# A transformer and state-space layer: its feed-forward network by seven products of quarter blocks, with normed input and stored activations

## The chip, the core and the metric

The kernel runs on one core of a Trainium2 chip. The metric is the device time of one execution in microseconds; lower is better.

## The reference

One layer on 1024 tokens with 1024 channels, all in fp32. Attention heads and a state-space (SSD) mixer run side by side, and their outputs are projected back and added to x. Then comes the feed-forward part, which is what the change touches:

```
x = x + jnp.concatenate([y_ssd, y_att], axis=-1) @ w_out[l]
h = rms_norm(x, norm2_w[l])
x = x + (jax.nn.silu(h @ w_gate[l]) * (h @ w_up[l])) @ w_down[l]
```

`w_gate` and `w_up` are 1024 x 2816, `w_down` is 2816 x 1024; 2816 is 22 tiles of 128.

## The kernel before

Channels lie on the 128 partitions, tokens along the free dimension. A matrix operand in fp32 is taken as a sum of two fp32r numbers: a high part, which ScalarE copies (line 136 for weights), and a low part, the difference of the two, by VectorE or GpSimd (line 137). A product is then three matmuls: high by high, high by low, low by high. `mm3` (lines 142 to 147) does that for both halves of 512 tokens at once, in six matmuls of 128x512 into two PSUM banks.

Attention runs to about 545 us, the SSD mixer to about 860, and the output projection to about 1004. Its eight tiles of 128 channels are added by `add_out` and `add_last`, and its operands are split by `split_y` (lines 887 and 888). `out_post` adds the two banks to x in `x2[d]` (lines 996 and 997), and ScalarE and GpSimd sum the squares (line 1005). As each `x2[d]` is done, it is multiplied by the norm's weight and split into `xh` and `xl` (lines 1015 and 1016), not yet by the norm's factor, which hangs on all channels.

In the feed-forward part `gate_up(f)` makes one tile of 128 of the 2816 channels: 8 tiles of x, gate and up, so 16 `mm3` and 96 matmuls. The factor of the norm (`norm2`, made while the first tile runs) goes on the products when they leave PSUM (lines 1050 and 1052). VectorE and ScalarE then form silu(gate) times up, and split it in turn (lines 1054 and 1055). `down(f0, n, ...)` multiplies four such tiles (two in the last part) with `w_down` and adds to `x2`: 8 output tiles of 6n matmuls. Parts are interleaved so that a `down` has the next `gate_up` ahead of it. The last output tile goes in columns of 512, 256 and 256 (`tail`, line 1059). GpSimd does nothing here after the norm's power (line 100).

A scheduler of the compiler sets the order of instructions on each engine from the program's order and from when its model takes operands to be ready; pools with a given number of buffers (`bufs`) make a writer wait for the readers of an older tile. Loads of weights are issued by SyncE (SP); loads of x by GpSimd (line 989).

Of the kernel before, what the change touches and what calls it, by code (L numbers as in the profile page):

```python
# [24 lines left out]
FF_PARTS = [(0, 4), (4, 4), (8, 4), (12, 4), (16, 4), (20, 2)]  # L25
# [40 lines left out]
def layer(ctx, tc, xT, wq0, wqkv, wxz, wout, wgu, wdn, pk, pb, cst, rot, sel, out):  # L66
# [44 lines left out]
    def row_a(spread):  # L111
        for i in range(2):
# [9 lines left out]
    def row_b(bank, spread, dst):  # L122
        for i in range(2):
# [760 lines left out]
    def split_y(src, pl_, tag, eng):  # L884
        yh = pl_.tile([P, S], F32R, tag=tag, name="yh", bufs=16)
        yl = pl_.tile([P, S], F32R, tag=tag, name="yl", bufs=16)
        A.copy(out=yh, in_=src)
# [299 lines left out]
```

## Time and profile before

| | |
|---|---|
| median of 3 runs | 1730.51 us (1730.05 to 1730.52) |
| the profiled execution | 1730.91 us, of which the span is 1729.1 |
| TensorE matmul (PE) | 1692.8 us busy (98%), 8614 matmuls |
| VectorE (DVE) | 956.2 us (55%) |
| ScalarE (ACT) | 679.2 us (39%) |
| GpSimd (POOL) | 443.7 us (26%) |
| moved by DMA | 93.5 MB, mean 54 GB/s |

The span is the profiled part of one execution; 1.8 us lie around it. Busy shares are means over the whole span; what a change does is read from the stretches that it touches. The mean duration of a matmul in the groups, some 393 ns, is the time from its start to its end, and matmuls overlap in the engine: the pace is read from how many go by in a stretch.

### The profile page before, as it was taken

Reading aid. Unit: us, or ns where it says so; the run is one execution under the profiler, and the core shown is the slowest. Engines: PE = TensorE matmul, PEld = TensorE weight load, DVE = VectorE, ACT = ScalarE, POOL = GpSimd, SP = SyncE. Lnnn points to the kernel's source line nnn. Section 1 sums busy time; section 2 is a strip of 40 time slices with the busy share of each in tenths; the row PEclk is TensorE's granted clock in tenths of the full one; section 3 lists DMA queues with packets and bytes.
Section 4 is the critical chain, followed back from the end, with each engine's and each line's share of the span. In section 5 each row is a group of like instructions: output and inputs, shape, how many; then the busy total and the mean of one; then the engine's idle time right before and its main releaser. Section 6 shows DMA issues by size and latency. Waiting matters only on the chain.

```text
span 1729.1 us, 23256 instructions
## 1 busy us (share of the span) xinstructions
PE 1692.8 (98%) x8614; PEld 1445.6 (84%) x8614; DVE 956.2 (55%) x1969; ACT 679.2 (39%) x1517; POOL 443.7 (26%) x678
## 2 busy tenths in 40 slices
PE   7899999999999999999999999999999999999999
PEld 7799999999988787887778788888888888888887
DVE  7788888878886577877531333333333333333334
ACT  5576666666664445447221322112112112212211
POOL 5755665566511334334242100000000000000000
PEclk8899999999999999999999999999999999999999
DMA  5100110111011111132141111111111111111112
GB/s 183 38 25 26 49 44 22 35 49 32 13 42 35 47 37 37 52 132 98 50 146 46 46 49 44 36 61 49 37 56 49 43 56 49 43 50 49 49 48 112
DMA packets 50033, 93.50 MB, mean 54 GB/s; under 512 B 5738, under 2 KB 14442, under 8 KB 49920
## 3 DMA queue, kind: packets, MB, share of 16 engines
q1 hardware_dynamic: 39024, 82.44, 14.5%
q10 hardware_dynamic: 9504, 4.72, 1.0%
q0 software_dynamic: 1392, 4.85, 0.8%
q8 instruction: 68, 1.11, 0.3%
q14 instruction: 45, 0.37, 0.1%
HBM read 81.51 MB, written 10.49 MB: 53 GB/s over the span
## 4 chain that ended last, share of the span: by engine, by line
PE 67%; DVE 1%; POOL 0%; issue 0%; ACT 0%; DVEq 0%; POOLq 0%
PE p L142 9%; PE p L143 9%; PE p L147 9%; PE p L145 9%; PE p L144 8%; PE p L146 8%; PE ps_x L461 4%; PE ps_x L462 4%; PE ps_x L463 4%; PE ps_y L797 1%; PE ps_n L775 1%; PE ps_o L813 1%; PE ps_d L752 1%; PE ps_xt L741 0%; DVE yl L888 0%
## 5 line engine op out<-in xcount | busy, mean ns | idle before, releaser
L136 ACT CAST wh<-wr 128x512 fp32r<-128x512 f32 (+3 forms) x237 | 153.1, 647 | 708.6 <-PE p L145 604.1
L137 DVE TENSOR_TENSOR wl<-wr,wh 128x512 fp32r<-128x512 f32 (+1 forms) x175 | 130.1, 743 | 274.7 <-ACT wh L136 274.7
L184 PE MATMUL ps_pj<-wh,xwh 128*128 128x384 f32 (+1 forms) x512 | 176.1, 347 | 6.9 <-ACT wh L136 6.1
L186 PE MATMUL ps_pj<-wh,xwl 128*128 128x384 f32 (+1 forms) x512 | 174.2, 342 | 3.9 <-DVE xwl L251 3.9
L185 PE MATMUL ps_pj<-wl,xwh 128*128 128x384 f32 (+1 forms) x512 | 174.4, 341 | 0.0
L137 POOL TENSOR_TENSOR wl<-wr,wh 128x512 fp32r<-128x512 f32 (+3 forms) x62 | 101.8, 1642 | 236.0 <-ACT wh L136 229.0
L142 PE MATMUL p<-xh,wh 128*128 128x512 f32 x352 | 138.6, 394 | 0.7 <-DVE x L996 0.7
L143 PE MATMUL p<-xl,wh 128*128 128x512 f32 x352 | 138.8, 394 | 0.0
L144 PE MATMUL p<-xh,wh 128*128 128x512 f32 x352 | 138.6, 394 | 0.0
L145 PE MATMUL p<-xl,wh 128*128 128x512 f32 x352 | 138.3, 393 | 0.0
L147 PE MATMUL p<-xh,wl 128*128 128x512 f32 x352 | 138.3, 393 | 0.0
L146 PE MATMUL p<-xh,wl 128*128 128x512 f32 x352 | 137.7, 391 | 0.0
L461 PE MATMUL ps_x<-xwh,wh 128*128 128x512 f32 x320 | 129.2, 404 | 0.8 <-ACT ya L405 0.8
L462 PE MATMUL ps_x<-xwl,wh 128*128 128x512 f32 x320 | 126.2, 394 | 0.0
L463 PE MATMUL ps_x<-xwh,wl 128*128 128x512 f32 x320 | 125.7, 393 | 0.0
L359 ACT ACTIVATE pt<-ps_s,nm 128x640 f32<-128x640 f32 (+7 forms) x128 | 94.3, 740 | 45.1 <-DVE nm L354 26.3
L184 PEld LDWEIGHTS ps_pj<-wh,xwh 128*128 128x128 f32 x512 | 97.8, 191 | 7.7 <-ACT wh L136 7.2
L186 PEld LDWEIGHTS ps_pj<-wh,xwl 128*128 128x128 f32 x512 | 97.5, 191 | 5.0 <-DVE xwl L251 4.9
L185 PEld LDWEIGHTS ps_pj<-wl,xwh 128*128 128x128 f32 x512 | 97.6, 191 | 0.8 <-POOL wl L137 0.4
L354 DVE TENSOR_REDUCE nm<-ps_s 128x1 f32<-128x640 f32 (+7 forms) x128 | 93.4, 744 | 1.2
L1082 DVE TENSOR_TENSOR x<-p,x 128x512 f32<-128x512 f32 x47 | 32.1, 689 | 110.3 <-PE p L146 110.3
L142 PEld LDWEIGHTS p<-xh,wh 128*128 128x128 f32 x352 | 66.1, 188 | 15.6 <-ACT wh L136 1.4
(238 smaller groups left out, 3850.0 us busy)
## 6 DMA issues: line engine op xcount, KB each, us to landing
wr<-in_wgu_dram SPq DMA_DIRECT2D x88, 256.0 KB, 2.7
wr<-in_wdn_dram SPq DMA_DIRECT2D x44, 256.0 KB, 2.7
wr<-in_wqkv_dram SPq DMA_DIRECT2D x28, 384.0 KB, 3.1
wr<-in_wxz_dram SPq DMA_DIRECT2D x40, 256.0 KB, 2.7
wr<-in_wout_dram SPq DMA_DIRECT2D x32, 256.0 KB, 2.8
big<-yd SPq DMA_DIRECT2D x10, 512.0 KB, 3.8
yd<-ya ACTq DMA_DIRECT2D x64, 64.0 KB, 1.7
x<-in_xT_dram POOLq DMA_DIRECT2D x8, 512.0 KB, 6.3
```

Source lines behind the costliest of these rows:

```text
L137: lo_eng.tensor_tensor(out=wl[:, cs], in0=wr[:, cs], in1=wh[:, cs], op=ALU.subtract)
L142: T.matmul(out=ps0, lhsT=wh, rhs=ah[:, 0:512], start=first, stop=False)
L143: T.matmul(out=ps0, lhsT=wh, rhs=al[:, 0:512], start=False, stop=False)
L144: T.matmul(out=ps1, lhsT=wh, rhs=ah[:, 512:1024], start=first, stop=False)
L145: T.matmul(out=ps1, lhsT=wh, rhs=al[:, 512:1024], start=False, stop=False)
L146: T.matmul(out=ps0, lhsT=wl, rhs=ah[:, 0:512], start=False, stop=last)
L147: T.matmul(out=ps1, lhsT=wl, rhs=ah[:, 512:1024], start=False, stop=last)
L184: T.matmul(out=ps[:, :n], lhsT=xwh[k][:, ts], rhs=wh[:, k % 2, :], start=k == first, stop=False)
L185: T.matmul(out=ps[:, :n], lhsT=xwh[k][:, ts], rhs=wl[:, k % 2, :], start=False, stop=False)
L186: T.matmul(out=ps[:, :n], lhsT=xwl[k][:, ts], rhs=wh[:, k % 2, :], start=False, stop=k == last)
L461: T.matmul(out=ps, lhsT=wh[:, ks], rhs=xwh[k][:, fs], start=k == 0, stop=False)
L462: T.matmul(out=ps, lhsT=wh[:, ks], rhs=xwl[k][:, fs], start=False, stop=False)
```

## The change

A product of two 2x2 block matrices takes eight products of blocks. The change does it in seven (`PRODUCTS`), with four sums of weight blocks and four of data blocks formed beforehand, and the seven results added up into the four blocks of the output. For gate and up the blocks are: data, the halves of the tokens by the halves of the channels (a11, a12, a21, a22); weights, gate and up by the halves of the channels. For the down product: halves of the tokens by the two tiles of a pair, and two output tiles.

- **x normed first.** Only normed x can be summed. The output projection's last two tiles are done for the first half of the tokens, then for the second, with their weights loaded twice; after each half `norm2(hf)` makes the factor, multiplies eight tiles of x by it (line 1059) and splits them (`split`, lines 152 and 153). x before the norm is stored to DRAM (`x2d`).
- **Two tiles plainly, twenty by seven products.** Tiles 0 and 1 go as before, one half after the other, while GpSimd forms the sums of x (lines 1077 to 1083). `GateUp` does a tile in seven products of 12 matmuls. GpSimd forms the four sums of weights (line 1151); VectorE forms the low halves and, with ScalarE, adds up the results.
- **Activations through DRAM.** `store_pair` writes three quarters of each pair of activation tiles and four sums of them (GpSimd, lines 1096 to 1102) to `md`, 77 blocks of 256 KB.
- **The down product last, in four chunks** of 3, 3, 3 and 2 pairs. A chunk has four steps, one for each pair of output tiles, of 7 products with 3n matmuls each. `fetch_m` loads the blocks of a chunk (line 1264) into four buffers `mr` and splits them; `Ahead` does it for the next chunk between the products of the last step. The sums start from x, loaded from `x2d` (line 1325).

```diff
-FF_PARTS = [(0, 4), (4, 4), (8, 4), (12, 4), (16, 4), (20, 2)]
+NPLAIN = 2
+CHUNKS = [(0, 3), (3, 3), (6, 3), (9, 2)]
+PRODUCTS = ["a11", "s2", "s1", "s3", "a12", "s4", "a22"]
+BANKS = "abcdacd"
...
+    def split(op, src, eng, n=512):
+        A.copy(out=op[:, 0:n], in_=src)
+        eng.tensor_tensor(out=op[:, n : 2 * n], in0=src, in1=op[:, 0:n], op=ALU.subtract)
+        return op
...
-    def mm3(ps0, ps1, wh, wl, ah, al, first, last):
+    def mm3(ps, wh, wl, a, first, last, more=False):
+        T.matmul(out=ps, lhsT=wh, rhs=a[:, 0:512], start=first, stop=False, skip_group_check=more)
+        T.matmul(out=ps, lhsT=wh, rhs=a[:, 512:1024], start=False, stop=False, skip_group_check=more)
+        T.matmul(out=ps, lhsT=wl, rhs=a[:, 0:512], start=False, stop=last, skip_group_check=more)
...
+            for hf in range(2):
+                for d in range(DK - 2, DK):
+                    for hq in range(4):
+                        add_out(d, hq // 2, hq % 2, (hf,))
+                jobs.append((lambda ws, hf=hf: norm2(hf), []))
...
+    def out_post(d, hf):
+        fs = halves[hf]
+        V.tensor_tensor(out=x2[d][:, fs], in0=pd.pop((d, hf)), in1=x2[d][:, fs], op=ALU.add)
+        nc.sync.dma_start(out=x2d[d, :, fs], in_=x2[d][:, fs])
...
+    def norm2(hf):
...
+        row_b(bank, [sx], accm[:, fs])
+        for d in range(DK):
...
+            V.scalar_tensor_tensor(out=x2[d][:, fs], in0=x2[d][:, fs], scalar=nw, in1=accm[:, fs], op0=ALU.mult, op1=ALU.mult)
+            name = f"a{1 + hf}{1 + d // 4}"
+            op = (rb if name in ("a11", "a22") else ra).tile([P, S], F32R, tag=name, name=name, bufs=4)
+            ops[(name, d % 4)] = split(op, x2[d][:, fs], V)
...
+    def store_pair(i):
...
+        G.tensor_tensor(out=s3, in0=m0[:, 0:512], in1=m0[:, 512:1024], op=ALU.subtract)
+        put("s3", s3)
...
     while jobs:
         half()
+    for f, u, hf, last in ((0, 0, 0, 0), (0, 1, 0, 0), (1, 0, 0, 0), (0, 0, 1, 1), (0, 1, 1, 1), (1, 0, 1, 1), (1, 1, 0, 0), (1, 1, 1, 1)):
+        if (f, u, hf) == (0, 1, 1):
...
+                    ops[(name, k)] = split(op, src, V)
+        plain(f, u, hf, last)
...
+    class Weights:
...
+                G.tensor_tensor(out=self.t[name], in0=x, in1=y, op=ALU.subtract)
...
+    class GateUp:
...
+        def product(self, j):
...
+            ps, w = self.ps[BANKS[j]], self.parts[j]
+            for k in range(4):
+                mm3(ps, w[:, k * P : (k + 1) * P], w[:, 512 + k * P : 512 + (k + 1) * P], ops[(PRODUCTS[j], k)], k == 0 and j < 4, k == 3, j > 3)
...
+            elif j == 5:
+                m = m_tile(self.f)[:, halves[0]]
+                add(m, self.u)
+                V.tensor_tensor(out=m, in0=m, in1=self.g0, op=ALU.mult)
+            else:
+                g1 = mq.tile([P, 512], F32, tag="gt", name="gt", bufs=2)
+                add(g1, self.u)
+                A.activation(g1, g1, AF.Silu)
+                V.tensor_tensor(out=m_tile(self.f)[:, halves[1]], in0=self.up1, in1=g1, op=ALU.mult)
...
+    def run(steps):
...
+        for n, st in enumerate(steps):
+            for j in range(7):
+                st.product(j)
+                if n + 1 < len(steps):
+                    steps[n + 1].prepare(j)
+                if n + 2 < len(steps) and j in (3, 6):
+                    steps[n + 2].load((0, 1) if j == 3 else (2, 3))
+            st.end()
...
+    def fetch_m(c, j):
+        p0, n = CHUNKS[c]
+        for i in range(n):
+            mr = wd.tile([P, 512], F32, tag="mr", name="mr", bufs=4)
+            nc.gpsimd.dma_start(out=mr, in_=md[p0 + i, j])
+            mo[(c, j, i)] = split(rd.tile([P, S], F32R, tag="op", name="mo", bufs=24), mr, V)
...
+    class Down:
...
+            wr = wd.tile([P, 3, 4, P], F32, tag="wr", name="wr", bufs=2)[:, : self.n]
+            nc.sync.dma_start(out=wr, in_=wdn[self.p0 : self.p0 + self.n, self.d].rearrange("i p (q n) -> p i q n", n=P))
...
+            A.copy(out=op[:, 0], in_=src)
+            V.tensor_tensor(out=op[:, 1], in0=src, in1=op[:, 0], op=ALU.subtract)
...
+            for i in range(self.n):
+                mm3(ps, w[:, 0, i], w[:, 1, i], mo[(self.c, j, i)], i == 0 and j < 4, i == self.n - 1, j > 3)
...
+    for j in range(7):
+        fetch_m(0, j)
     for d in range(DK):
...
+        nc.gpsimd.dma_start(out=acc[d], in_=x2d[d])
+
+    class Ahead(Down):
+
+        def product(self, j):
+            super().product(j)
+            if not self.last:
+                fetch_m(self.c + 1, j)
+
+    run([(Ahead if d == DK // 2 - 1 else Down)(c, d) for c in range(len(CHUNKS)) for d in range(DK // 2)])
```

**TensorE where the feed-forward begins.** Before (`xh`, `xl`: split x; `wh`, `wl`: split weights; `yh`: the projection's operand; `p`: a PSUM bank):

```order
L147 MATMUL p_10364<-yh,wl 128x512
L142 MATMUL p_10523<-xh,wh 128x512
L143 MATMUL p_10523<-xl,wh 128x512
L144 MATMUL p_10524<-xh,wh 128x512
L145 MATMUL p_10524<-xl,wh 128x512
L146 MATMUL p_10523<-xh,wl 128x512
L147 MATMUL p_10524<-xh,wl 128x512
L142 MATMUL p_10523<-xh,wh 128x512
```

After, at the second half (`op`: split weights; `a`: split x, high and low in one tile):

```order
L166 MATMUL p_10683<-a_10409,op 128x512
L117 MATMUL ps_tr<-cst_sb,wide 40x128
L135 MATMUL ps_bc<-sx,ones_r 128x512
L164 MATMUL p_10710<-a_10568,op 128x512
L164 MATMUL p_10805<-a_10568,op 128x512
L164 MATMUL p_10831<-a_10568,op 128x512
L165 MATMUL p_10710<-a_10568,op 128x512
L166 MATMUL p_10710<-a_10568,op 128x512
```

Before, the first matmul on x follows the last of the projection. Now a transpose and a broadcast of the norm's factor stand between them, and three tiles take turns with the second half of x as its tiles come.

**VectorE at the same place.** Before:

```order
L996 TENSOR_TENSOR x_7_9725<-p_10363,x_7_9725 128x512
L997 TENSOR_TENSOR x_7_9725<-p_10364,x_7_9725 128x512
L137 TENSOR_TENSOR wl<-wr,wh 128x512
L1016 SCALAR_TENSOR_TENSOR xl<-x_7_9725,pk_sb,xh 128x1024
L137 TENSOR_TENSOR wl<-wr,wh 128x512 x2
L99 TENSOR_SCALAR rtok<-ps_r_10573 128x8
L105 COPY wide<-rtok 128x2x8
```

After (`sx`: the factor's spread rows; `m`: an activation tile; `accm`: the factor on all partitions):

```order
L123 TENSOR_TENSOR sx<-wrow,cst_sb 40x512
L1122 TENSOR_TENSOR m<-p_10646,gt 128x512
L1059 SCALAR_TENSOR_TENSOR x_0_9701<-x_0_9701,pk_sb,accm 128x512
L1059 SCALAR_TENSOR_TENSOR x_1_9703<-x_1_9703,pk_sb,accm 128x512
L1059 SCALAR_TENSOR_TENSOR x_2_9705<-x_2_9705,pk_sb,accm 128x512
L1059 SCALAR_TENSOR_TENSOR x_3_9707<-x_3_9707,pk_sb,accm 128x512
L1059 SCALAR_TENSOR_TENSOR x_4_9709<-x_4_9709,pk_sb,accm 128x512
L1059 SCALAR_TENSOR_TENSOR x_5_9711<-x_5_9711,pk_sb,accm 128x512
L1059 SCALAR_TENSOR_TENSOR x_6_9713<-x_6_9713,pk_sb,accm 128x512
L1059 SCALAR_TENSOR_TENSOR x_7_9715<-x_7_9715,pk_sb,accm 128x512
L153 TENSOR_TENSOR a_10568<-x_0_9701,a_10568 128x512
```

Before, only the last tile's addition and its low half stand ahead of that first matmul, and the norm comes behind. Now all eight tiles are normed first, and the first low half (line 153) comes behind the eighth.

**GpSimd from the output projection to the end, and from gate-up to down.** Before, its last rows:

```order
L1005 TENSOR_TENSOR accm<-accm,sq_10351 128x512
L1005 TENSOR_TENSOR accm<-accm,sq_10354 128x512
L1005 TENSOR_TENSOR accm<-accm,sq_10469 128x512
L1005 TENSOR_TENSOR accm<-accm,sq_10472 128x512
L100 TENSOR_TENSOR rtok<-rtok,mhalf 128x8
L1183 UNCONDITIONAL_BRANCH
L1183 ISA
```

After, where gate-up passes to down (`sd`: the last activation sum; `mr`: an activation block; `acc`: x to add to; `t`: a weight sum):

```order
L1102 TENSOR_TENSOR sd<-m,sd 128x512
L1264 DMA mr<-md 128x512 x4
L1325 DMA acc_13880<-x2d 128x1024
L1325 DMA acc_13881<-x2d 128x1024
L1325 DMA acc_13882<-x2d 128x1024
L1325 DMA acc_13883<-x2d 128x1024
L1325 DMA acc_13884<-x2d 128x1024
L1325 DMA acc_13885<-x2d 128x1024
L1325 DMA acc_13886<-x2d 128x1024
L1325 DMA acc_13887<-x2d 128x1024
L1151 TENSOR_TENSOR t<-wr 128x384
L1264 DMA mr<-md 128x512 x4
```

Before, there is nothing for it in the feed-forward part. Now the issue of the first block loads stands behind the last sum, four can go, eight loads of x come next, and the other blocks stand behind these.

## Rows read from the trace of the kernel before

Groups of lines give engine, operation, out<-in, form and count, then busy us, mean ns of one, and idle us just before with what ended most of it. Chains and timelines give start us, us, and what.

**Rows 1.** Windows: output projection, a feed-forward stretch, the end.

```profile
core 0: us, PE busy (x) PEld busy (x) DVE busy (x) ACT busy (x) POOL busy (x), PEclk, DMA share, GB/s
870.00:980.00 110.00, 110.00 (x480) 89.99 (x479) 24.27 (x30) 27.82 (x40) 31.07 (x26) 1.00 0.24 81
1112.47:1245.15 132.68, 132.68 (x577) 108.50 (x577) 46.22 (x72) 24.71 (x40) 0.00 (x0) 1.00 0.15 48
1643.66:1729.10 85.44, 81.66 (x360) 66.75 (x359) 32.98 (x53) 9.90 (x16) 0.00 (x0) 1.00 0.22 80
```

**Rows 2.** Waits of PE after 780 us: us, times, longest us.

```profile
PE p L143 <- POOL yl L888: 1.3, 1, 1.3
PE p L142 <- DVE x L996: 0.7, 1, 0.7
```

**Rows 3.** Chain that ended last, around 862 us (start us, us, what).

```profile
861.27 1.06 ACT yh L887
862.40 3.47 POOL yl L888
```

**Rows 4.** Groups by line and form: busy us, mean ns | idle before.

```profile
L463 PE MATMUL ps_x<-xwh,wl 128*128 128x512 f32 x320 | 125.7, 393 | 0.0
L1055 DVE TENSOR_TENSOR ml<-ut,mh 128x512 fp32r<-128x512 f32 x44 | 28.5, 689 | 1.9
L845 DVE SCALAR_TENSOR_TENSOR big<-big,pk_sb,accg 128x1024 f32<-128x1024 f32 x8 | 11.9, 1542 | 6.2 <-ACT accg L126 6.2
L136 ACT CAST wh<-wr 128x512 fp32r<-128x512 f32 x204 | 126.2, 620 | 705.4 <-PE p L145 604.1 <-PE ps_x L462 49.1 <-issue 13.7
L989 POOL DMA_DIRECT2D x<-in_xT_dram x8 | 4.4, 554 | 2.6 <-DVE yl L888 2.6
L299 POOL TENSOR_TENSOR raw<-raw,w_qk 128x192 f32<-128x192 f32 x56 | 41.1, 734 | 76.5 <-ACT raw L298 45.8 <-issue 29.7 <-POOL klo L336 0.9
```

**Rows 5.** Timeline and groups, 600 to 800 us: DVE beside POOL.

```profile
649.18 2.54 POOL L757 TENSOR_TENSOR mt<-mt,cbt 128x512 f32<-128x512 f32 x2 [0.45 <-ACT mt L756]
650.82 1.45 DVE L137 TENSOR_TENSOR wl<-wr,wh 128x512 fp32r<-128x512 f32 x1 [2.43 <-ACT wh L136]
...
L822 DVE TENSOR_TENSOR big<-big,eac 128x384 f32<-128x384 f32 x7 | 6.2, 884 | 0.2
L821 DVE TENSOR_TENSOR eac<-ps_o,eac 128x384 f32<-128x384 f32 x7 | 3.9, 555 | 0.0
```

**Rows 6.** Line 137 from 1112 to 1643 us: duration ns min/median/max.

```profile
L137 DVE TENSOR_TENSOR wl<-wr,wh x96: 680/691/696, 1124.3 to 1637.7; 128x512 fp32r<-128x512 f32 x96
```

**Rows 7.** Windows around a wait near 32 us, columns as rows 1.

```profile
30.00:32.00 2.00, 0.81 (x3) 0.48 (x3) 2.00 (x1) 0.83 (x1) 1.63 (x1) 1.00 0.09 37
32.00:34.00 2.00, 0.04 (x1) 0.04 (x1) 2.00 (x3) 0.00 (x0) 0.00 (x0) 0.88 0.60 190
34.00:36.00 2.00, 2.00 (x6) 1.99 (x7) 1.92 (x2) 0.00 (x0) 0.00 (x0) 0.50 0.03 10
40.00:45.00 5.00, 5.00 (x20) 4.96 (x19) 4.15 (x17) 1.76 (x5) 4.89 (x12) 0.62 0.00 0
```

**Rows 8.** Chain around the start of the feed-forward.

```profile
1003.83 1.68 PE ps_r L98 x16
1016.78 0.66 PE ps_bc L125 x2
```

**Rows 9.** DMA issues (KB each, median us to landing), and a window.

```profile
wr<-in_wgu_dram SPq DMA_DIRECT2D x88, 256.0 KB, 2.7
x<-in_xT_dram POOLq DMA_DIRECT2D x8, 512.0 KB, 6.3
out_dram<-x SPq DMA_DIRECT2D x2, 128.0 KB, 2.1
sel_f<-in_sel_dram POOLq DMA_DIRECT2D x2, 120.0 KB, 2.8
...
10.00:15.00 5.00, 5.00 (x28) 4.77 (x27) 4.26 (x9) 4.62 (x6) 4.89 (x9) 1.00 1.04 408
```

More of the change, by code (lines that the diff above doesn't have):

```diff
@@ L111, in row_a @@
     def row_a(spread):
-        for i in range(2):
+        for i in range(len(spread)):
             V.tensor_tensor(
@@ L882, in add_last, with split_y @@
         jobs.append((run, pcs))
[L884 to L887, printed above, removed]
-        eng.tensor_tensor(out=yl, in0=src, in1=yh, op=ALU.subtract)
-        return yh, yl
+    def split_y(src, kk, eng):
+        tags = (("a21", "s1"), ("a12", "s3"), ("a22", "s4"), ("a11", "s2"))[kk // 4]
+        return [
+            split((ra if kk < 8 else rb).tile([P, S], F32R, tag=tag, name="y", bufs=4), src[:, 512 * hf : 512 * hf + 512], eng)
+            for hf, tag in enumerate(tags)
+        ]
     def fetch(dst, i):
@@ new lines, in layer, with m_tile, sums @@
+    ms = {}
+    def m_tile(f):
+        if f not in ms:
+            ms[f] = mq.tile([P, S], F32, tag="m", name="m", bufs=2)
+        return ms[f]
+    def sums(a, b, c, d, t):
+        G.tensor_tensor(out=t, in0=a, in1=c, op=ALU.subtract)
+        yield "s3", t
+        G.tensor_tensor(out=c, in0=c, in1=d, op=ALU.add)
+        yield "s1", c
+        G.tensor_tensor(out=a, in0=c, in1=a, op=ALU.subtract)
+        yield "s2", a
+        G.tensor_tensor(out=b, in0=b, in1=a, op=ALU.subtract)
+        yield "s4", b
@@ new lines, in layer, with plain @@
+    plain_w, plain_p = {}, {}
+    def plain(f, u, hf, last):
+        if (f, u) not in plain_w:
+            plain_w[(f, u)] = [load_op(wgu[f, u, :, 512 * i : 512 * i + 512], G if i else V) for i in range(2)]
+        ps = psum[0].tile([P, 512], F32, tag="acc", name="p0", bufs=4)
+        for k in range(DK):
+            op = plain_w[(f, u)][k // 4]
+            mm3(ps, op[:, (k % 4) * P : (k % 4 + 1) * P], op[:, 512 + (k % 4) * P : 512 + (k % 4 + 1) * P], ops[(f"a{1 + hf}{1 + k // 4}", k % 4)], k == 0, k == DK - 1)
+        if last:
+            del plain_w[(f, u)]
+        if u == 0:
+            gt = mq.tile([P, 512], F32, tag="gt", name="gt", bufs=2)
+            A.activation(gt, ps, AF.Silu)
+            plain_p[(f, hf)] = gt
+        else:
+            V.tensor_tensor(out=m_tile(f)[:, halves[hf]], in0=ps, in1=plain_p.pop((f, hf)), op=ALU.mult)
@@ new lines, in layer @@
+    run([GateUp(f) for f in range(NPLAIN, NFF)])
+    wbctx.close()
+    rctx.close()
+    ac = pool(ctx, "ac")
+    acc = [ac.tile([P, S], F32, name=f"acc{d}") for d in range(DK)]
+    ua = [ac.tile([P, 512], F32, name=f"ua{d}") for d in range(DK // 2)]
+    wd = pool(ctx, "wd")
+    rd = pool(ctx, "rd", side="right")
+    mo = {}
+    def fetch_m(c, j):
[4 more added lines that the diff above has]
+            mo[(c, j, i)] = split(rd.tile([P, S], F32R, tag="op", name="mo", bufs=24), mr, V)
```

303 lines of the change are left out of this document (189 added, 114 removed).

## The prediction

> **What bounds the kernel now.** I read the windows first, since the change touches only what comes after 860 us. In the output projection TensorE is busy for all of the 110 us, at a granted clock of 1.00, with VectorE at 24 us and GpSimd at 31; in the feed-forward stretch it is busy for all of 132.68 us, with VectorE at 46, ScalarE at 25 and GpSimd at nothing; only the last stretch has 3.8 us at its end without it [rows 1]. The waits say the same: after 780 us TensorE waits once for 1.3 and once for 0.7 us [rows 2]. So the matmuls set the time, each that goes saves its place in the queue, and each wait put in costs in full. The pace is 132.68 / 577 = 0.230 us for a 128x512 matmul [rows 1]; the 393 ns of the groups [rows 4] is not that.
>
> **Matmuls.** A gate-up tile takes 96 before and 7 x 12 = 84 after, 19.3 us at 0.230; twenty tiles save 240. Down takes 22 x 48 = 1056 before and 4 x 11 x 7 x 3 = 924 after: 132 saved. 372 x 0.230 = **-85.6 us**. All of it is on the path, since TensorE never waits there now.
>
> **Inside gate-up: nothing added.** The other engines have 19.3 us a tile. VectorE: seven low halves and two multiplications at 0.69 [rows 4, 6], five additions from PSUM at no more than that: 9.7. ScalarE: seven copies and three more at 0.62 [rows 4]: 6.2. GpSimd: four weight sums and two activation sums. Its row of 192 columns is 0.73 [rows 4], and two of 512 took 2.54, so 1.27 each [rows 5]: 7.6. A VectorE operation with two SBUF inputs seems to wait for GpSimd: beside that pair a low half took 1.45 us [rows 5] against 0.680 to 0.696 with GpSimd idle [rows 6], and at one size two SBUF inputs take 884 ns where one from PSUM takes 555 [rows 5]. Even if the two took strict turns (9 x 0.69 + 7.6 = 14), 19.3 covers it. Weights come 256 KB in 2.7 us [rows 9], two tiles ahead; the stores go in the same queue, 15 transfers of 256 KB for a pair of tiles, 38.6 us. If that cover goes (sums late, because they wait for VectorE), the next late thing is the low half of product s2, the first that needs two sums in a row.
>
> **Seam one, x normed first: +32.5.** Time zero is the last first-half product of tile 7. 96 second-half matmuls cover 22.1 us, with the factor's small matmuls 23.6. The last of the factor's steps, the broadcast, stands by the order among these, at 20.8; with 0.33 for it (0.66 for two [rows 8]) and a copy, at 21.7 eight multiplications begin, for which the nearest row is 1542 ns for 1024 columns [rows 4], so 0.77 each: 6.2. One GpSimd operation (1.27), a weight's and x's low half (0.69 each) bring the first operand to 30.6. With three matmuls more TensorE is through at 24.3: it waits 6.3. 43 matmuls then run 9.9 us, slower where the clock has fallen. A wait near 32 us let the granted clock fall from 1.00 to 0.50, that is 2.4 to 1.2 GHz, after TensorE had been busy for 0.81 of one 2 us window and 0.04 of the next; three windows of 2 us at 0.50 (one is shown) and 5 us at 0.62 lost 0.24 + 3 + 1.9 = 5 us [rows 7]. I count these 5 once. Then the second half: 16 small matmuls took 1.68 [rows 8], four and their way through VectorE, GpSimd, transpose and broadcast some 4 us, under 26 matmuls (6.0) that are still to do; then eight multiplications, two GpSimd operations (2.5) and a low half: from 51 to 62.8, a wait of 10.5 with three matmuls in it. Then nine low halves take turns with the sums of x, (0.69 + 1.27) x 9 = 17.6 for 36 matmuls (8.3) and three small gaps more: 8.5. The end of the sums and of the first weights' sums: 3. Today's wait of 0.7 [rows 2] goes. 6.3 + 5 + 10.5 + 8.5 + 3 - 0.7 = 32.6. If VectorE and GpSimd did not wait for each other, no GpSimd term and no 8.5 stand in it, and half of the clock's: 16. The beside-and-alone pair [rows 5, 6] speaks for the higher end, and I take 32.5.
>
> **Seam two, gate-up to down: +25.** After the last gate-up product come an addition, silu and a multiplication, 2.0, then three sums, 3.8: 5.9. Only behind them, by GpSimd's order, stand the first four loads of activation blocks: 0.55 to issue each (line 989) [rows 4], and landing after 2.8 (120 KB) to 6.3 us (512 KB) for GpSimd's queue [rows 9]; for 256 KB I take 4, then copy and low half: the first product at 12. Weights, 768 KB on SP, come with them. Next stand eight loads of x, 4 MB; at the 408 GB/s that the trace shows [rows 9] they take 10.3 us, and the second four blocks stand behind them: they land at 24. TensorE has 21 matmuls (4.8) for that time. The other 13 blocks come by fours, as `mr` has four buffers; a round is issue, landing, copy and low half, some 6 us (0.55 + 4 + 0.62 + 0.69). They feed the next 120 matmuls (27.6) at about TensorE's pace, from 24 to 28 on, so the first 141 end at some 56 in place of 141 x 0.230 = 32.5: 23.5, and I add 2 for the clock. Ends: 12 (loads of x don't hold the blocks back), 33 (landing at 6.3).
>
> **Chunk boundaries: +10.** A step of three pairs is 63 matmuls, 14.5 us. The block loads of the next chunk, 21 of them, are split on VectorE beside the last step: 7 additions at 0.56 (line 821) [rows 5], 7 weight low halves and 21 block low halves at 0.69. Over two steps TensorE has 29.0 us; VectorE 2 x 8.7 + 14.5 = 31.9, and up to 8.4 for GpSimd's eight weight sums, of 384 columns at some 1.05, an estimate between 0.73 and 1.27 [rows 4, 5]. The rounds of four at 6 us bring 18 blocks in 27 us, about the same window. So the boundaries are near balance: 0 if all is hidden, 22 if everything adds (VectorE's 2.9 and the 8.4 two or three times); 10 is 3 to 4 us for each of three.
>
> **The ends.** The last addition is of 512 columns, not 256 (+0.3), its store of 256 KB, 2.7 against 2.1 for 128 KB [rows 9]: +1. At 862 us the chain runs through a copy of 1.06 and a GpSimd difference of 3.47, both of 1024 columns [rows 3]; in halves the first is through earlier, and the wait of 1.3 [rows 2] goes: -1.3. Eight more weight pieces in the projection (0.62 and 0.69 each) lie under a stretch where VectorE is busy for 24 of 110 us [rows 1]. The stores, 16 of x and 77 of activations, 256 KB each, are waited for only where down begins; behind them in SP's queue are weights two tiles ahead. In the stretches shown the DMA share is 0.15 to 0.24 [rows 1]. If that cover goes, a late weight delays a whole tile.
>
> **Sum.** -85.6 + 32.5 + 25 + 10 + 1 - 1.3 = **-18.4**. The profiled execution took 1730.9, so 1712.5; it stands 0.4 above the median, so **1712 us**.
>
> **Rivals.**
>
> *Seams cheap, faster.* VectorE does not wait for GpSimd (seam one 16), the loads of x don't hold the blocks (12), boundaries 2: -85.6 + 16 + 12 + 2 = -56: **1675**. For it: TensorE's queue can take matmuls of other tiles in between; against: [rows 5, 6].
>
> *The clock falls at each gap.* My sum has 7 us for it. Five gaps of 6 us and more stand in the seams (two in the first, three in the second); if the loss of 5 us near 32 us comes after each, it is 25: **1730**, no change. Against: after a gap with more waits behind it, TensorE waits for operands at either clock. The Trainium skill, "TensorE: Matmul & The Clock Gate", section "HAM oscillation — how this bites in real kernels", says that matmuls after such a gap run at the lower clock anew each time; the trace agrees for one gap, with the 5 us [rows 7], and shows no row of several, and by it the sum would be -0.4.
>
> *Block loads too slow: slower.* One mechanism: four `mr` buffers, filled by GpSimd's queue and freed by VectorE. The 21 blocks of a chunk need more than five rounds. Each us that a round takes above 6 adds 4.5, 4.5 and 3 us at the boundaries (18, 18 and 12 blocks by fours) and 3.25 in the first chunk (13): 15.2. At 7.2 us the gain is gone; at 9 it is -18.4 + 46 = +27: **1757**. For it: GpSimd's loads land after 6.3 us for 512 KB [rows 9], and its issue stands behind its sums, which take turns with VectorE. Against: at 4 us for a landing a round is under 6. The Trainium skill, "SBUF — State Buffer", section "Who interferes with whom", infers that such VectorE operations hold only the reading side of the port that the two share, while writing a load's descriptors needs the other side, so the issue would not wait; no run here shows that, and by it the rival's price is that of landings alone, of the 6 us in a round 4.
>
> *Seven products take as long as eight*, if matmuls into one bank in a row were slower. Against: the projection of the SSD stage runs three matmuls in a row into one bank and shows 393 ns like the others (line 463) [rows 4]. It would leave the seams alone: **1798**.
>
> **How the numbers follow.** A change under 0.2%, 3.5 us, is about what a measurement can't tell from none. Forecast (1690 to 1727): 0.48; cheap seams 0.24; clock 0.07; slow loads 0.18; seven as eight 0.03. Faster: 0.46 of the forecast (0.02 of it lies at its upper edge), 0.24, and 0.04 of the clock: 0.74. Same: 0.02, 0.03 of the clock and 0.02 of slow loads at about 7 us a round: 0.07. Slower: 0.16 and 0.03: 0.19. The range from 1680 to 1742 leaves out some 0.1 below (cheap seams) and 0.1 above (rounds over 8 us); the upper end is a round of 8 us, +12.
>
> **What the profile would show.** Windows: gate-up tiles of 19.3 us at a busy share of 1.00. Waits of TensorE of about 6 and 10 us before the first products with normed x, released by VectorE; one of 12 and one of about 7 us where down begins, released by the split of a block whose load is late; three gaps of a few us at chunk ends. VectorE's low halves at 1.4 to 2 us beside GpSimd's sums, 0.69 else. The forecast is wrong if gate-up has waits, if seam one costs under 20 or over 40, or if block loads keep TensorE waiting throughout the chunks.

## The result and the profile after

The changed kernel takes **1708.34 us** (median of 4 runs, 1707.36 to 1708.81) against 1730.28 of the kernel before beside it: a ratio of 0.9875, 95% interval 0.9857 to 0.9892, so 1.25% faster. 1712 was forecast, with a range of 1680 to 1742. The time is right; several of its terms are not, and that they made up for one another was in part luck.

The page's first lines; the span went from 1729.1 to 1705.6 us, and VectorE, ScalarE and GpSimd have more to do:

```profile
span 1705.6 us, 23840 instructions
PE 1630.9 (96%) x8237; PEld 1383.0 (81%) x8237; DVE 1155.7 (68%) x2213; ACT 782.3 (46%) x1751; POOL 786.4 (46%) x988
```

The windows, by stage (columns as in [rows 1]): the projection up to the first matmul on normed x, the norm seam, gate-up, the seam to down, down, and the end.

```profile
858.62:993.41 134.79, 134.79 (x581) 108.53 (x581) 38.84 (x51) 35.55 (x60) 44.31 (x39) 1.00 0.35 121
993.40:1074.00 80.60, 64.31 (x248) 49.76 (x247) 62.67 (x66) 29.36 (x50) 50.02 (x28) 0.87 0.17 59
1074.00:1454.20 380.20, 380.20 (x1637) 307.99 (x1635) 205.68 (x270) 111.89 (x189) 157.70 (x113) 1.00 0.28 95
1454.20:1490.70 36.50, 14.23 (x31) 8.34 (x31) 17.91 (x22) 12.13 (x24) 23.61 (x31) 0.58 0.77 286
1490.70:1698.70 208.00, 207.93 (x895) 168.31 (x893) 172.90 (x277) 86.12 (x170) 107.57 (x134) 1.00 0.45 147
1698.70:1705.60 6.90, 0.00 (x0) 0.00 (x0) 0.69 (x1) 0.00 (x0) 0.00 (x0) 0.64 0.20 76
```

Gate-up and down run without a gap, as far as TensorE goes; all that is lost lies in two places of 80 and 36 us and in the last 7. In the place of the two waits of [rows 2], TensorE's waits from 990 to 1500 us:

```profile
PE ps_a L164 <- ACT mo L152: 14.8, 1, 14.8
PE p L165 <- DVE a L153: 8.9, 2, 5.0
PE ps_b L164 <- ACT op L1289: 4.2, 1, 4.2
PE ps_a L166 <- DVE op L1290: 2.4, 1, 2.4
PE p L164 <- ACT a L152: 2.1, 1, 2.1
PE ps_a L164 <- DVE m L1122: 1.6, 1, 1.6
PE ps_bc L135 <- DVE sx L123: 1.5, 1, 1.5
PE p L166 <- POOL op L153: 1.5, 1, 1.5
PE p L166 <- DVE op L153: 0.7, 1, 0.7
PE ps_b L166 <- DVE op L1290: 0.6, 1, 0.6
PE ps_a L165 <- DVE mo L153: 0.3, 1, 0.3
```

**The ledger.** A matmul takes 380.20 / 1637 = 0.2323 us in gate-up. By that pace the matmuls of each window need 134.8, 57.0 (238, and 1.7 for small ones), 380.2, 7.2 and 207.9: 787.1 in sum. Before, TensorE was busy for 865.6 us from the same point (857.8) to its last matmul. So:

| term | forecast | measured |
|---|---|---|
| matmuls | -85.6 | 787.1 - 865.6 = -78.5 |
| seam one (80.6 - 57.0, less 0.7 before) | +32.5 | +22.9 |
| seam two (36.5 - 7.2) | +25 | +29.3 |
| chunk boundaries | +10 | 0 |
| the end (6.9 against 3.8) | +1 | +3.1 |
| around 862 us, and up to it (858.6 against 857.8) | -1.3 | -0.4 |
| sum | -18.4 | -23.6 (spans: -23.5) |

Seam two in the timeline: the last gate-up product ends near 1454, and GpSimd's last sum starts at 1459.31.

```profile
1456.62 1.26 POOL L1098 TENSOR_TENSOR ss<-m 128x512 f32<-128x512 f32 x1 [18.22 <-DVE m L1225]
...
1459.31 1.26 POOL L1102 TENSOR_TENSOR sd<-m,sd 128x512 f32<-128x512 f32 x1
1460.86 2.20 POOL L1264 DMA_DIRECT2D mr<-md  x4 [0.30 <-POOL sd L1102]
1461.31 22.88 SPq L1277 DMA_DIRECT2D wr<-in_wdn_dram  x3
1463.05 2.62 POOL L1325 DMA_DIRECT2D acc<-x2d  x5
...
1468.11 0.51 ACT L1289 CAST op<-wr 128x384 fp32r<-128x384 f32 x1 [12.29 <-DMA wr<-in_wdn_dram]
1468.53 2.17 ACT L152 CAST mo<-mr 128x512 fp32r<-128x512 f32 x4
1469.19 0.80 PE L164 MATMUL ps_a<-mo,op 128*128 128x512 f32 x1 [14.82 <-ACT mo L152]
...
1473.86 0.54 POOL L1264 DMA_DIRECT2D mr<-md  x1 [1.36 <-DMA acc<-x2d]
1475.09 0.54 POOL L1264 DMA_DIRECT2D mr<-md  x1 [0.70 <-DMA acc<-x2d]
1476.37 0.54 POOL L1264 DMA_DIRECT2D mr<-md  x1 [0.74 <-DMA acc<-x2d]
1476.92 1.00 POOL L1151 TENSOR_TENSOR t<-wr,t 128x384 f32<-128x384 f32 x1
1478.53 0.80 PE L164 MATMUL ps_b<-mo,op 128*128 128x512 f32 x1 [4.19 <-ACT op L1289]
```

Blocks and weights are asked for at 1460.9 and 1461.3. ScalarE copies the weights first, 6.8 us later, and the blocks behind them. After that GpSimd issues block loads that wait for loads of x to land, and the second sum of the weights, which the second product needs, stands behind these at 1476.9.

### The profile page after: what moved, and what is told of

Same layout as the page of the kernel before. It is cut to its first block, busy times and chain, and to the rows that moved or that the text cites. A ratio compares the mean times of both kernels' runs of the same rounds, so it can differ in the third digit from the quotient of the medians.

```text
span 1705.6 us, 23840 instructions
## 1 busy us (share of the span) xinstructions
PE 1630.9 (96%) x8237; PEld 1383.0 (81%) x8237; DVE 1155.7 (68%) x2213; ACT 782.3 (46%) x1751; POOL 786.4 (46%) x988
## 4 chain that ended last, share of the span: by engine, by line
PE 86%; DVE 6%; issue 3%; ACT 2%; DMA 1%; POOL 1%; DVEq 0%; ACTq 0%; POOLq 0%
PE ps_pj L203 5%; PE ps_pj L205 5%; PE ps_pj L204 5%; PE ps_x L481 5%; PE ps_x L482 4%; PE ps_x L483 4%; PE p L166 4%; PE p L165 4%; PE p L164 3%; PE ps_c L164 3%; PE ps_a L166 3%; PE ps_c L165 3%; PE ps_d L166 3%; PE ps_c L166 3%; PE ps_d L164 3%; PE ps_d L165 3%
## 5 line engine op out<-in xcount | busy, mean ns | idle before, releaser
L152 ACT CAST op<-wr 128x512 fp32r<-128x512 f32 x148 | 91.2, 618 | 260.4 <-PE p L166 94.9
L153 DVE TENSOR_TENSOR op<-wr,op 128x512 fp32r<-128x512 f32 x104 | 85.6, 825 | 151.5 <-ACT op L152 143.6
L1151 POOL TENSOR_TENSOR t<-wr,t 128x512 f32<-128x512 f32 (+2 forms) x72 | 92.5, 1285 | 152.8 <-issue 123.7
L153 POOL TENSOR_TENSOR op<-wr,op 128x512 fp32r<-128x512 f32 x44 | 58.8, 1336 | 224.8 <-ACT op L152 224.8
L481 PE MATMUL ps_x<-xwh,op 128*128 128x512 f32 x320 | 129.8, 406 | 0.9 <-ACT ya L424 0.9
L482 PE MATMUL ps_x<-xwl,op 128*128 128x512 f32 x320 | 126.7, 396 | 0.0
L483 PE MATMUL ps_x<-xwh,op 128*128 128x512 f32 x320 | 126.5, 395 | 0.0
L1151 POOL TENSOR_TENSOR t<-wr 128x512 f32<-128x512 f32 (+2 forms) x72 | 87.9, 1221 | 62.9 <-DVE op L153 32.9
L166 PE MATMUL p<-y,op 128*128 128x512 f32 x256 | 101.3, 398 | 0.0
L165 PE MATMUL p<-y,op 128*128 128x512 f32 x256 | 101.2, 397 | 0.0
L152 ACT CAST op<-t 128x512 fp32r<-128x512 f32 x80 | 49.6, 622 | 111.4 <-PE ps_c L166 53.9
L164 PE MATMUL p<-y,op 128*128 128x512 f32 x256 | 99.5, 399 | 0.0
L153 DVE TENSOR_TENSOR op<-t,op 128x512 fp32r<-128x512 f32 x80 | 77.2, 967 | 31.9 <-ACT op L152 30.9
```

Of the source, the lines that this page charges most:

```text
L152: A.copy(out=op[:, 0:n], in_=src)
L153: eng.tensor_tensor(out=op[:, n : 2 * n], in0=src, in1=op[:, 0:n], op=ALU.subtract)
L164: T.matmul(out=ps, lhsT=wh, rhs=a[:, 0:512], start=first, stop=False, skip_group_check=more)
L165: T.matmul(out=ps, lhsT=wh, rhs=a[:, 512:1024], start=False, stop=False, skip_group_check=more)
L166: T.matmul(out=ps, lhsT=wl, rhs=a[:, 0:512], start=False, stop=last, skip_group_check=more)
L481: T.matmul(out=ps, lhsT=wh[:, ks], rhs=xwh[k][:, fs], start=k == 0, stop=False)
```

## The experiments

Medians are of 4 runs (10 for the two of the kernel before, 5 for the last). Kernels of one batch share the runs of the kernel before; ratios are to these.

| kernel | median us | ratio, 95% interval |
|---|---|---|
| changed | 1708.34 | 0.9875 (0.9857 to 0.9892) |
| b_bank | 1729.26 | 0.9997 (0.9988 to 1.0006) |
| b_xtile | 1730.84 | 1.0001 (0.9991 to 1.0010) |
| hl | 1710.02 | 0.9881 (0.9866 to 0.9896) |
| sums_v | 1704.34 | 0.9854 (0.9837 to 0.9870) |
| acc_late | 1707.82 | 0.9872 (0.9857 to 0.9886) |
| mr_sp | 1710.71 | 0.9886 (0.9871 to 0.9900) |
| acc_add | 1708.87 | 0.9873 (0.9857 to 0.9890) |
| acc_add_sp | 1700.74 | 0.9827 (0.9812 to 0.9841) |
| mr2 | 1722.12 | 0.9950 (0.9932 to 0.9968) |
| warm | 1703.22 | 0.9841 (0.9826 to 0.9855) |
| warm_v_sp | 1679.49 | 0.9704 (0.9687 to 0.9720) |
| warm_shift | 1658.91 | 0.9590 (0.9577 to 0.9603) |

### Why a matmul takes 0.2323 us

**Three in a row into one bank** (b_bank), in the kernel before:

```diff
         T.matmul(out=ps0, lhsT=wh, rhs=al[:, 0:512], start=False, stop=False)
+        T.matmul(out=ps0, lhsT=wl, rhs=ah[:, 0:512], start=False, stop=last)
         T.matmul(out=ps1, lhsT=wh, rhs=ah[:, 512:1024], start=first, stop=False)
         T.matmul(out=ps1, lhsT=wh, rhs=al[:, 512:1024], start=False, stop=False)
-        T.matmul(out=ps0, lhsT=wl, rhs=ah[:, 0:512], start=False, stop=last)
```

> The kernel before, with the six matmuls of a pair put in the order of the change: three in a row into one bank, then three into the other, in place of turns between two banks. Theory one: three in a row into one bank (with the weights switched three times as often per two banks) run at 0.2323 us each, as in the changed kernel, in place of 0.2298; 3168 matmuls of the feed-forward part and 768 of the output projection then take 9 to 10 us longer, about 1740 us. Theory two: the slower pace of the changed kernel comes from its other engines or from its operand layout, high and low halves in one tile: no change, 1730 us, pace 0.2298.

Theory two: no change. From 1112.47 to 1245.15 us 577 matmuls go by, as in the kernel before [rows 1].

**High and low in one tile** (b_xtile), in the kernel before, for x and the activations:

```diff
-        xh = ra.tile([P, S], F32R, tag="ta", name="xh", bufs=16)
-        xl = ra.tile([P, S], F32R, tag="ta", name="xl", bufs=16)
+        for hf in range(2):
+            xa = ra.tile([P, S], F32R, tag="ta", name="xa", bufs=16)
```

> The kernel before with its moving operands of the feed-forward part in the layout of the change: high and low half of 512 columns in one tile of 1024, a tile for each half of the tokens, in place of a tile of high and one of low values. Theory one: the slower pace of the changed kernel, 0.2323 us a matmul against 0.2295 in groups of 65, is due to that layout: 3168 matmuls take 8 us longer, about 1738 us, and the intervals are 0.2323. Theory two: it is the layout of the weights or something else: no change, 1730 us, intervals 0.2295.

Theory two again: 578 in the same stretch.

**Weights in two tiles** (hl), in the changed kernel:

```diff
+    def op_tile(p, bufs):
+        return HL(p.tile([P, 512], F32R, tag="oph", name="oph", bufs=bufs), p.tile([P, 512], F32R, tag="opl", name="opl", bufs=bufs))
...
-        return split(wb[0].tile([P, S], F32R, tag="op", name="op", bufs=6), wr, eng)
+        return split(op_tile(wb[0], 6), wr, eng)
```

> The changed kernel with the split weights of the output projection and of gate-up in two tiles of 512 columns, one of high and one of low values, in place of both in one tile of 1024. Theory one: the slower pace, 0.2323 us a matmul in place of 0.2295, comes from the layout of the weights; some 768 + 1872 matmuls are 2.8 ns shorter each: 7 us less, 1701 us, intervals 0.2295 in gate-up and 0.2323 still in down. Theory two: it comes from something else, such as where the tiles begin: 1708 us, intervals 0.2323.

Theory two: 0.2323 in gate-up. That left the place of the tiles. In the kernel before, groups of 24 matmuls, each on one piece of weights, take turns between two paces; in the changed kernel all are alike (mean us from start to start, from the traces; before from 1150.13 us, where a gate-up tile begins, changed from 1200.22):

```
before       0.2329 0.2275 0.2329 0.2275 0.2329 0.2275 0.2325 0.2275
changed      0.2329 0.2321 0.2325 0.2325 0.2321 0.2325 0.2321 0.2329
```

In the compiled programs the split weights begin at addresses that leave these remainders when divided by 256, while the split x and activations leave 224 in all three:

```
before       wh, wl  3200 bytes apart    96 and 224 in turns
changed      op      4096 bytes apart    96
warm_shift   op      4096 bytes apart    224
```

In the kernel before a gate-up tile begins with a piece at 96, so the slower groups are those at 96. A whole gate-up tile has 0.2302; the 0.2295 of the expectations is from 65 or 66 matmuls, which are no whole number of turns. The weights of hl are all at 96 too, though in two tiles. warm_shift, the last kernel below, moves the weights by 128 bytes and tests it.

### Seam one: VectorE beside GpSimd

sums_v:

```diff
-        G.tensor_tensor(out=t, in0=a, in1=c, op=ALU.subtract)
+        V.tensor_tensor(out=t, in0=a, in1=c, op=ALU.subtract)
```

and so for the other three sums of x.

> The changed kernel with the sixteen sums of x at the norm seam on VectorE in place of GpSimd. Theory one: VectorE's operations with two SBUF inputs wait for GpSimd's; with GpSimd silent they take 0.69 us, the eight low halves of the second half come without turns, and though VectorE has 16 x 0.69 = 11 us more work, the seam is 3 to 6 us shorter: 1703 us. Theory two: the long durations are no waits for GpSimd; then VectorE has 11 us more on the path and the seam is 6 to 10 us longer: 1716 us.

Theory one. The low halves at the seam, on VectorE (duration ns min/median/max), in the changed kernel:

```profile
L153 DVE TENSOR_TENSOR s<-x,s x12: 1114/1763/1779, 1036.2 to 1061.0; 128x512 fp32r<-128x512 f32 x12
L153 DVE TENSOR_TENSOR a<-x,a x8: 681/682/683, 1028.3 to 1033.7; 128x512 fp32r<-128x512 f32 x8
```

and in sums_v:

```profile
L153 DVE TENSOR_TENSOR s<-x,s x12: 678/682/684, 1033.9 to 1049.6; 128x512 fp32r<-128x512 f32 x12
```

The same twelve operations take 1763 ns beside GpSimd's sums and 682 without them, as [rows 5, 6] had it; from 993.4 to 1074 TensorE gets 277 matmuls in place of 248, which is 6.7 us. The median is 4 us lower; the intervals of the two ratios overlap, so the rows carry the verdict. (In the profiled run the first wait of seam two is 18.0 in place of 14.8, though nothing was changed there.)

The row of the eight `a` shows that these were not disturbed even in the changed kernel. It was GpSimd that stood still: the first of its additions, which overwrite x and so come behind the first of these low halves, took 6.43 us, the longest of four:

```profile
L1079 POOL TENSOR_TENSOR x<-x,x x4: 1292/1739/6428, 1029.1 to 1048.6; 128x512 f32<-128x512 f32 x4
```

VectorE's turns came only under the `s`, and TensorE had matmuls on the `a` to do meanwhile.

### Seam two: loads of x, queues, a cold start

**x by SP** (acc_late):

```diff
-    for d in range(DK):
-        nc.gpsimd.dma_start(out=acc[d], in_=x2d[d])
...
+            if self.c == 0:
+                for d in (2 * self.d, 2 * self.d + 1):
+                    nc.sync.dma_start(out=acc[d], in_=x2d[d])
```

> The changed kernel with the eight loads of x for the down sums issued by SP, two behind the weights of each of the first four steps, in place of GpSimd's queue. Theory one: what makes the second half of the gate-up-to-down seam is GpSimd's order, where block loads and weight sums stand behind loads of x that must land; the waits of 4.2, 2.4 and 0.6 us go and part of the slow clock with them: 6 to 12 us less, about 1698 us. Theory two: the 4 MB of x fill the DMA engines whichever queue issues them: within 2 us of the changed kernel, 1708.

No gain, as theory two has it: the first wait is 16.2, and others came in the place of the 4.2. The first wait differs by some 3 us between kernels that leave this place alone (14.8 in the changed kernel, 17.1 in hl, 18.0 in sums_v), so 16.2 is neither more nor less than before.

**x later** (acc_add): the first chunk's sums are copied, x is added in the second.

```diff
+            if self.c == 1 and j == 6:
+                for i in range(2):
+                    a = acc[2 * self.d + i]
+                    G.tensor_tensor(out=a, in0=a, in1=self.x[i], op=ALU.add)
```

> The changed kernel with the 4 MB of x not loaded at the start of the down product: the first chunk's results are copied out of PSUM, and x is loaded beside the second chunk's weights and added by GpSimd. Theory one: in the seam from gate-up to down the DMA engines are full (328 and 409 GB/s in two windows of 10 us), and x takes what blocks and weights wait for; without it some 2.5 MB stand ahead of the first products, the first wait falls from 14.8 to about 12 us and the later ones of 4.2, 2.4 and 0.6 go: 10 to 14 us less, 1694 to 1698 us. Theory two: the seam is set by the rounds of four block buffers and by the weight sums on GpSimd, not by the DMA engines: at most 3 us less, 1705 us.

No gain: the first wait is 16.7 (TensorE's waits from 1440 us on), and waits of 5.1, 2.6 and 1.9 follow. Two tiles of x were still loaded at the start, since nothing held them back, so theory one is not quite excluded; but with 1 MB of x in place of 4 the wait did not fall below the 14.8 to 18.0 of the others.

**Blocks by SP** (mr_sp), and all three together (acc_add_sp):

```diff
-            nc.gpsimd.dma_start(out=mr, in_=md[p0 + i, j])
+            nc.sync.dma_start(out=mr, in_=md[p0 + i, j])
```

> The changed kernel with the 77 activation blocks loaded by SP in place of GpSimd's queue; the loads of x stay with GpSimd. Theory one: GpSimd's weight sums stand behind block loads that wait for a buffer; freed of them, the seam loses its second and third waits, some 7 us, and the 4.5 us between the last store's landing and the end of the span shrink to the 1.8 of the kernel before if they belong to GpSimd's queue: 1698 to 1701 us. Theory two: SP's weight loads then stand behind blocks that wait for buffers, and the chunk ends show waits of TensorE: 1710 to 1725 us.

> As acc_add, with the sums of x at the norm seam on VectorE as in sums_v and the activation blocks loaded by SP as in mr_sp. If the three gains are separate (seam two 10 to 14 us, seam one 4, the end 3): 1687 to 1692 us. If SP's order, in which weights stand behind blocks that wait for buffers, takes back the first, as the first wait of 24.8 us in mr_sp suggests: 1697 to 1704 us.

mr_sp has its first wait at 24.8, and its time is in the range of theory two, but not by the mechanism of theory two: TensorE has no wait after 1500 us, so none at a chunk end, and SP issues the first weights right behind four blocks:

```profile
1462.08 4.27 POOL L1325 DMA_DIRECT2D acc<-x2d  x8
1462.89 2.05 SPq L1264 DMA_DIRECT2D mr<-md  x4
1464.99 1.15 SPq L1277 DMA_DIRECT2D wr<-in_wdn_dram  x2
...
1480.15 0.51 ACT L1289 CAST op<-wr 128x384 fp32r<-128x384 f32 x1 [4.93 <-DMA wr<-in_wdn_dram]
```

The weights are copied 15.2 us after they are asked for, against 6.8 in the changed kernel. GpSimd, with no blocks to issue, asks for all eight tiles of x, 4 MB, between 1462.1 and 1466.4; from 1465 to 1480 us the DMA engines move 379 to 408 GB/s (398 to 410 in the changed kernel). That x is what held the weights back is the likely reading, and was not tested by itself. The end shrinks, as theory one had it. acc_add_sp came out in the middle of its second case, 7.6 us under the changed kernel: about what sums_v (4) and the end (3) give, and little else.

**Memory that gate-up has done with** (warm): the four tiles of a21 hold the first weights (`w0`) and the block buffers (`mrs`).

```diff
+    mrs = [ra.tile([P, S], F32, tag="a21", name="mr", bufs=4) for _ in range(2)]
+    w0 = [ra.tile([P, S], F32, tag="a21", name="w0", bufs=4) for _ in range(2)]
     wbctx.close()
-    rctx.close()
...
-            mr = wd.tile([P, 512], F32, tag="mr", name="mr", bufs=4)
+            mr = mrs[k // 2][:, halves[k % 2]]
...
-            op = wd.tile([P, 2, 3, P], F32R, tag="op", name="op", bufs=10)[:, :, : self.n]
+            op = wd.tile([P, 2, 3, P], F32R, tag="op", name="op", bufs=8)[:, :, : self.n]
```

> The changed kernel with buffers for the first weights and the first activation blocks of the down product in memory that gate-up no longer uses (the four tiles of the second half's first channels), so that these are loaded, and the first blocks split, while the last gate-up tile runs; the split blocks lie in the tiles of the seven operands, and the last pair's sums in a tile that is done. Eight weight buffers in place of ten. Theory one: the seam from gate-up to down is a cold start, since weights and blocks are asked for only when gate-up's memory comes free; the first wait falls from 14.8 to under 5 us, and the slow clock after it goes in part: 10 to 18 us less, 1690 to 1698 us. Theory two: the seam is set by what comes after, GpSimd's weight sums at 1.0 to 1.3 us for the first steps and the loads of x: the wait only moves, and under 5 us is won, 1704 us or more.

Half of each: 5.1 us less. The first wait is 7.1, and a second of 11.4 has come:

```profile
PE ps_b L164 <- ACT op L1302: 11.4, 1, 11.4
PE ps_a L164 <- ACT op L1302: 7.1, 1, 7.1
```

GpSimd's timeline says why: the sum for the second product waits behind eight loads of x and block loads that must see them land.

```profile
1461.66 3.14 POOL L1341 DMA_DIRECT2D acc<-x2d  x6
1465.65 0.53 POOL L1341 DMA_DIRECT2D acc<-x2d  x1 [0.84 <-DMA mr<-md]
1468.22 0.53 POOL L1341 DMA_DIRECT2D acc<-x2d  x1 [2.04 <-DMA mr<-md]
...
1472.77 0.54 POOL L1269 DMA_DIRECT2D mr<-md  x1 [1.49 <-DMA acc<-x2d]
1474.31 0.54 POOL L1269 DMA_DIRECT2D mr<-md  x1 [1.00 <-DMA acc<-x2d]
1474.86 1.00 POOL L1152 TENSOR_TENSOR t<-w,t 128x384 f32<-128x384 f32 x1
```

**Both at once** (warm_v_sp): warm, with the edits of sums_v, mr_sp and acc_late.

> As warm, with the sums of x on VectorE as in sums_v, the blocks loaded by SP as in mr_sp, and x loaded by SP beside the weights as in acc_late. If the gains add (10 to 18 for the warm start, 4 for seam one, 3 at the end): 1683 to 1691 us. If blocks on SP hold back weights, it shows waits of TensorE in the first chunk, and 1693 to 1700 us.

Better than either case: 28.9 us under the changed kernel, where the gains of the four edits alone come to 7 (5.1, 4.0, 0.5 and -2.4). TensorE's waits from 1440 us on are these two:

```profile
PE ps_a L164 <- ACT op L1309: 7.1, 1, 7.1
PE ps_a L166 <- DVE op L1310: 0.5, 1, 0.5
```

So seam two was two delays in a row: the cold start (the first weights and blocks are asked for only when gate-up is through) and GpSimd's queue. warm shortened the first and left the second to be met; acc_late and mr_sp took loads out of GpSimd's queue and left the cold start. Whether beside warm the move of x or that of the blocks counts for more was not tried.

### The rounds of block buffers (mr2)

```diff
-            mr = wd.tile([P, 512], F32, tag="mr", name="mr", bufs=4)
+            mr = wd.tile([P, 512], F32, tag="mr", name="mr", bufs=2)
```

> The changed kernel with two buffers for activation blocks in place of four. Theory one, the slow case of the prediction: rounds set the chunk ends; a round of two takes some 5 us (issue 0.54, landing 3.2, copy 0.62, low half 0.69), 18 blocks 45 us against a window of 29, so TensorE waits 10 to 16 us at each of three boundaries and 10 in the first chunk: 1735 to 1760 us. Theory two: VectorE, busy for 29.7 of 30 us there, sets them, and two buffers keep it fed: under 5 us more, 1713 us.

In between: 14 us more. From 1490 to 1640 us TensorE waits for blocks, 9.2 us in sum, of which the two longest rows are:

```profile
PE ps_c L164 <- ACT mo L152: 4.0, 2, 2.7
PE ps_a L165 <- DVE mo L153: 1.7, 2, 1.3
```

Rounds can set the chunk ends, but only with half the buffers, and then at 14 us where I gave 27 to 52.

### The place of the weights (warm_shift)

```diff
             wb.append(pool(wbctx, "wb"))
+            wb[0].tile([P, 32], F32, name="gap")
...
+    ac.tile([P, 32], F32, name="gap2")
     wd = pool(ctx, "wd")
```

> As warm_v_sp, with an unused tile of 128 bytes ahead of the split weights, so that these begin 128 bytes further on (also in the down product). In the kernel before, groups of 24 matmuls take 0.2283 and 0.2321 us a matmul in turns, as weights come from buffers that lie 3200 bytes apart, which is 128 more than a multiple of 256; in the changed kernel all weights lie at multiples of 256 from one another, and all matmuls take 0.2323. Theory one: the place of the weights within 256 bytes sets the pace; all are now at the other place, and 960 + 768 + 2796 matmuls take 0.2283: up to 18 us less, 1661 to 1670 us. Theory two: the turns in the kernel before come from its moving operands, or something else: 1679 us and 0.2323.

Theory one, and more: 20.6 us less. From 1100 to 1400 us, in gate-up, warm_v_sp:

```profile
1100.00:1400.00 300.00, 300.00 (x1293) 243.23 (x1292) 160.27 (x215) 91.38 (x154) 129.33 (x94) 1.00 0.30 102
```

and warm_shift:

```profile
1100.00:1400.00 300.00, 300.00 (x1325) 248.51 (x1324) 166.10 (x221) 93.94 (x158) 128.18 (x94) 1.00 0.29 101
```

1325 matmuls in place of 1293, at the same granted clock; in groups of 24 they start 0.2267 us apart, all alike, faster than the 0.2283 that the expectation took. The pace before, 0.2302 over a whole gate-up tile, lies half-way between its groups at 96 and at 224. **This kernel, 1658.91 us, beats both**: 2.9% under the changed one.

## Why the prediction was right, and where it was not

The sum was 5 us off. Its terms were too low by 14 us in all (matmuls, seam two, the end, the place around 862 us) and too high by 20 (seam one, chunk boundaries), so the closeness of the sum is in part luck; the way there, matmuls saved less what two seams cost, was right.

- **Matmuls, -85.6: mis-sized, -78.5.** The count was right and so was "seven as eight" at 0.03. The pace of 0.230 was a mean of two paces, and the change put every weight at the slower one. The argument on three matmuls in a row into one bank was sound (b_bank); the cause lay in addresses, which no row shows. (After 780 us TensorE waited four times, not twice; the other two, 0.7 and 0.2 us, lie ahead of 860 us and of the change.)
- **Inside gate-up, nothing: right.** 380.2 us without a gap.
- **Seam one, +32.5: too high, +22.9.** The first wait was 3.9 us (6.3 said; it is one of the two in the row of 8.9). The second came in three parts, 1.5 on the factor's way, 2.1 and 5.0, together 8.6 (10.5 said; the steps listed from 51 on end near 61, not at 62.8, so up to 2 us of this was a slip of the sum). The step that failed is that "nine low halves take turns with the sums of x", 8.5, and the 3 for the end of the sums: the rows of 1.6, 1.5 and 0.7, 3.8 us, are all there was, since the eight `a` went ahead undisturbed. (Its sum, 17.6 less 8.3, is 9.3 and not 8.5; and the lower end of 16 comes to 17.8 by its own terms.) That GpSimd's sums stretch VectorE's low halves, as priced, is shown by sums_v. The clock took more than the 5: 23.6 lost, less 16.3 of waits (3.9, 8.6 and 3.8), leaves 7.3.
- **Seam two, +25: near, +29.3.** Start, queue and order were as told; the first product came later (1469.2, 15 us after the last of gate-up; 12 said). That the 4 MB of x set the second half was right in part: x stands in GpSimd's queue ahead of blocks and weight sums, but without it there (acc_late), or with 1 MB of it (acc_add), the seam was no shorter: the cold start was still there. Waits sum to 22.3, so the clock took 7.0 where I gave 2; it was granted at 0.50 here:

```profile
1460.00:1480.00 20.00, 6.10 (x11) 3.13 (x11) 5.82 (x6) 5.19 (x11) 13.05 (x21) 0.50 0.97 368
```

- **Chunk boundaries, +10: wrong, 0.** VectorE is as near to balance as was said, busy for 29.71 of the 30 us from 1530 to 1560, but TensorE did not wait:

```profile
1530.00:1560.00 30.00, 30.00 (x131) 24.33 (x130) 29.71 (x49) 16.69 (x32) 17.08 (x24) 1.00 0.65 202
```

  A block lands after 3.2 us by the median, not 4, so a round is 5 us. I put balance down as half a loss, though the next chunk's blocks are ahead of their use by up to a step.
- **The end, +1: +3.1**, from a cost that I had not listed (below).
- **Rivals.** The mechanism of the slow one is real by mr2, but four buffers kept clear of it. The clock fell anew at the gaps of both seams: it was granted at 0.57 from 1000 to 1005 us and at 0.50 from 1025 to 1035 and from 1460 to 1480. That cost 14.3 us beside the waits, between my 7 and the rival's 25. The Trainium skill, "TensorE: Matmul & The Clock Gate", section "HAM oscillation — how this bites in real kernels", has matmuls after such waits run at the lower clock each time, and these rows agree in kind.

## What to carry to other kernels

Fewer matmuls pay in full only while TensorE is never kept waiting; where a kernel passes from one phase to the next, count what can be asked for before the old phase's memory is free, and lift all delays that stand in a row before judging one of them. Where the pace of equal matmuls differs between two kernels or takes turns within one, compare the addresses of their operands: here an unused 128 bytes was worth nearly as much as the whole change, 20.6 us against 21.9.

## What the runs showed that I had not expected

- **The place of the weights.** With moving operands (x and activations) at 224, split weights at addresses that leave 96 when divided by 256 run at 0.2323 us a 128x512 matmul, those that leave 224 at 0.2267. Whether it is the place of the weights or its distance from that of the moving operands was not tried. The attention projections of the kernel before suggest that the moving operand counts too. There x, at 224, is the operand that is loaded, and weights of 384 columns move, at 96 and 224 in turns: a group of three matmuls mostly takes 0.53 us with the moving weights at 96 and 0.52 with them at 224.
- **The end of the span.** The last rows of VectorE in the changed kernel and in mr_sp:

```profile
1698.74 0.69 DVE L1308 TENSOR_TENSOR acc<-ps_d,acc 128x512 f32<-128x512 f32 x1 [0.69 <-PE ps_d L166]
```

```profile
1705.38 0.69 DVE L1308 TENSOR_TENSOR acc<-ps_d,acc 128x512 f32<-128x512 f32 x1 [0.71 <-PE ps_d L166]
```

With the blocks on GpSimd's queue the span (1705.6) ends 6.2 us after that row; with them on SP's (1709.2) 3.1 after, as in the kernel before (3.3). Over all kernels it is 5.2 to 6.2 in the seven with the blocks on GpSimd's queue and 3.0 to 3.2 in the four with them on SP's. The stores land as soon in both, 2.0 us by the median; what goes on in those 3 us the profile does not show.
